# Modulation dot products placed behind residuals and scaled halves, handed out differently, and a softplus on 128 by 192

## The chip, the core and the metric

The kernel runs on one core of one Trainium2 chip. The metric is the device time in microseconds (us) of one execution. A core has TensorE (matrix products, written PE in the profile; PEld is its weight load), VectorE (DVE), ScalarE (ACT), GpSimd (POOL) and SyncE (SP, which here only issues DMAs). Each engine works through its own queue in order.

## The reference, cut to what matters

Two layers work on 384 tokens of width 1024 (128 context tokens, 256 latent ones), all in float32. In outline, for each layer:

```python
shift1, scale1, gate1, shift2, scale2, gate2 = split(silu(c) @ w_ada + b_ada, 6)   # c_ctx for context tokens
h = rms_norm(x, g1) * (1 + scale1) + shift1
z, xbc, dt_raw, p, u, v, gates = split(h @ w_in)
dt = softplus(dt_raw + dt_bias)                  # 2 directions x 32 heads = 64 rows
merged = sum of sigmoid(gate) * branch over (ssd(xbc, dt, z), pool(p), gmlp(u, v))
x = x + gate1 * (merged @ w_out)
h2 = rms_norm(x, g2) * (1 + scale2) + shift2
f_gate, f_up = split(h2 @ w_ffn_in)
x = x + gate2 * ((silu(f_gate) * f_up) @ w_ffn_out)
```

At the end there is one more RMS norm. The state-space scan (ssd) works in chunks of 128 tokens and also returns its final states.

## The kernel before

**Weights.** Every large product takes its weights in keys: blocks of 128 by 1024 floats, 512 KB, stored in the order of use. A key is loaded into one of RB = 6 buffers `raw` (L99), split by ScalarE into a rounded part `whi` (L116) and by VectorE into the rest `wlo` (L117), and used in three matmuls for each product (high by high, high by low, low by high; L166 to L168 where weights stand still, L461 to L463 where tokens do). `Flow.prepare` splits up to LEAD = 3 keys ahead, and `Flow.load` loads as far ahead as the six buffers let it. All loads go through SyncE's queue.

**Modulation.** silu(c) @ w_ada is 6144 columns for each layer. They are worked out as dot products on VectorE. A step is one key of transposed w_ada and two dot products on it (`ada`, L302, one for c_ctx and one for c; the profile calls the output `ajunk`). Eight steps make one of the six sections of a layer (0 shift1, 1 scale1, 2 gate1, 3 shift2, 4 scale2, 5 gate2). Sections 0 and 1 of layer one are worked out at the start by other code; 80 steps are left, and they wait in the list `adaq`. `take(n)` puts the next n steps into the flow of work, between the units of matmuls. Places where it is called:

- the states stage (`ssd`): 12 steps in layer one, 8 in layer two
- the mixers: 13 in layer one, 8 in layer two
- each pair of gate and up products of the FFN (`fi` keys): one step a pair, ten pairs in each half of the FFN
- the FFN's output (`fo` keys), by `between`: one step after each key but the last. Each half of the FFN has two blocks of output columns (q = 0, 1); the first half has 6 keys a block, the second half 5, of which four go as one unit in the last block of layer one.

So steps 1 to 25 lie in layer one's states and mixers, 26 to 35 in the first half of its FFN products, 36 to 45 in the first half of its FFN output, 46 to 55 and 56 to 60 in the second half; 61 to 68 lie in layer two's states, 69 to 76 in its mixers, 77 to 80 in its FFN.

**Order of the queues.** TensorE's order is the order of the program. The queues of the other engines are laid out by the compiler's planner, which goes through planned time and gives each engine the ready instruction of highest priority, by place in the program. `high_priority(offset=20)` moves an instruction forward by 20 places; `residual`, `scaled` and `norm` have it, `prepare` moves by 1. A dot product whose load is planned to have landed can thus be put in front of work that comes earlier in the program but isn't ready in the plan.

**The ends of a block.** After the last key of an output block, `residual` multiplies each of the three 128-token tiles by its gate row (`res`) and adds it to x (`accx`), two VectorE instructions a tile, which also frees the tile's PSUM buffer (four of tag `mm`). `scaled` takes the sum of squares (ScalarE), then a reciprocal root of about ten small VectorE instructions (`ssy`, `ssh`, `rst`), then multiplies x by it in two halves, tile `k`: the first on VectorE (L155), the second on ScalarE. `norm` transposes `k` on TensorE (L405), modulates it (`hf`) and splits it into `hthl`, which the next products read. The norms of tiles 1 and 2 are written into the middle of the first product of the next stage (the FFN's first block, or the second layer's V block).

**dt.** `dt_unit` projects dt. Its weight columns stand twice, so that PSUM rows 0 to 63 and 64 to 127 hold the same 64 rows. The softplus is worked out on rows 0 to 63 of 384 tokens: bias, Abs and Exp on ScalarE, then on VectorE a maximum, a reciprocal (L745), a polynomial of nine products, and the sum `dtt`. The two scans (L762, L763) follow.

Of the kernel before, what the change touches and what calls it, by code (L numbers as in the profile page):

```python
# [1 line left out]

# [1 line left out]

# [7 lines left out]
BF16 = mybir.dt.bfloat16  # L12
I32 = mybir.dt.int32
ACTF = mybir.ActivationFunctionType
ALU = mybir.AluOpType
# [4 lines left out]
D = 1024  # L20
NT = 3
TOK = 384
# [9 lines left out]
CP_G1, CP_G2, CP_CW, CP_CB, CP_DS, CP_GS, CP_PS, CP_GU, CP_DTB, CP_AL, CP_BA = 0, 8, 16, 136, 160, 176, 192, 200, 208, 209, 210  # L32
# [29 lines left out]
class Flow:  # L62


    def __init__(self, tc, nc, wdram, pool):
        self.tc, self.nc, self.wdram, self.pool = tc, nc, wdram, pool
        self.units = []
# [56 lines left out]
class Net:  # L124
    def __init__(self, ctx, tc, io):
        self.ctx, self.tc, self.nc, self.io = ctx, tc, tc.nc, io
        self.late = []
        self.tick = 0


    def t(self, pool, tag, shape, bufs, dtype=F32):
# [13 lines left out]
        self.nc.scalar.activation(out=out, in_=in_, func=func, **kw)  # L145

    def tt(self, out, a, b, op):
        self.nc.vector.tensor_tensor(out=out, in0=a, in1=b, op=op)  # L148

    def stt(self, out, a, s, b, op0, op1):  # L150
        self.nc.vector.scalar_tensor_tensor(out=out, in0=a, scalar=s, in1=b, op0=op0, op1=op1)  # L151

    def ts(self, out, a, s1, op0, s2=None, op1=None):
        if op1 is None:
            self.nc.vector.tensor_scalar(out=out, in0=a, scalar1=s1, scalar2=None, op0=op0)  # L155
        else:
            self.nc.vector.tensor_scalar(out=out, in0=a, scalar1=s1, scalar2=s2, op0=op0, op1=op1)

    def split(self, hi, lo, x):
        self.nc.scalar.copy(out=hi, in_=x)  # L160
# [131 lines left out]
    def ada(self, l, sec):  # L292

        hold = {}

        def step(k):
            def fn(raw):
                if k == 0:
                    hold["m"] = self.t(self.base, f"mod{sec}", [128, KT, 2], 2)
                for n in range(2):  # L300
                    junk = self.t(self.base, "ajunk", [128, D], 1, BF16)
                    self.nc.vector.tensor_tensor_reduce(out=junk, in0=raw, in1=self.crow[:, n, :], scale=0.5, scalar=0.0,  # L302
                                                        op0=ALU.mult, op1=ALU.add, accum_out=hold["m"][:, k, n:n + 1])
                if k == KT - 1:
                    self.ada_end(l, sec, hold["m"])
            return fn

        return [((l, sec), [("ada", l, sec, k)], step(k)) for k in range(KT)]
# [73 lines left out]
    def scaled_(self, i, q):  # L382

        r = self.squares(self.x[:, i, q * 512:(q + 1) * 512], D, ("x", i), q, self.parts)
        if q == 0:
            return
        xn = self.xnorm[i] = self.t(self.pool, "k4", [128, D], 4)
        self.ts(xn[:, 0:512], self.x[:, i, 0:512], r, ALU.mult)
        self.act(xn[:, 512:1024], self.x[:, i, 512:1024], ACTF.Copy, scale=r)

    def norm(self, l, which, i):
# [238 lines left out]
    def ssd(self, l):  # L630
        F = self.flow
        F.add([], lambda: self.ssd_open(l))
        self.main([("dt", l)], lambda w: self.dt_unit(l, w))
        fill = [("u", 0, c) for c in range(KT)] + [("g", br, c) for br in range(3) for c in range(KT)][:3 * KT - ORDER.count("g")]
        def filler(n):
            for _ in range(n):
                if fill:
                    kind, br, c = fill.pop(0)
                    if kind == "u":
                        self.main([("in", l, C_U + 128 * c)], lambda w, c=c: self.u_spill(l, c, w))  # L640
                    else:
                        self.main([("in", l, C_G + D * br + 128 * c)], lambda w, br=br, c=c: self.gate_spill(l, br, c, w))
        for g in range(4):
            self.main([("in", l, C_B + 128 * g)], lambda w, g=g: self.conv_unit(l, 16 + g, w))
            self.main([("in", l, C_C + 128 * g)], lambda w, g=g: self.conv_unit(l, 20 + g, w))
            if g == 0:
                self.post(L_TURN, lambda: self.turn(0))
                self.post(L_TURN2, lambda: self.turn(1))
            self.post(L_CB, lambda g=g: self.cb_unit(l, g))
            filler(FILL[g][0])  # L650
            for t in range(4 * g, 4 * g + 4):
                self.main([("in", l, C_X + 128 * t)], lambda w, t=t: self.conv_unit(l, t, w))
                self.post(L_DEC, lambda t=t: self.decay(l, t))
                self.post(L_XN, lambda t=t: self.xnat(l, t))
                self.post(L_ST, lambda t=t: self.states(l, t))
                self.post(L_Y, lambda t=t: self.ypair(l, t))
                self.take((t % 2 == 1) + (l == 0 and t % 4 == 2))
                self.main([("in", l, C_Z + 128 * t)], lambda w, t=t: self.z_unit(l, t, w))
                if t < 15:
                    filler(FILL[g][1 + t % 4])  # L660
            if g == 3:
                break
            self.post(L_G1, lambda g=g: self.gnorm1(l, g))
            self.post(L_G2, lambda g=g: self.gnorm2(l, g))
            for cc in range(4):
                self.post_main(L_SP + cc, [("brs", l, g, cc)], lambda w, g=g, cc=cc: self.sproj(l, g, cc, w))
        while self.late and len(fill) > T_G1 + T_G2 + T_G3:
            filler(1)
        self.flush_all()
        filler(len(fill) - T_G2 - T_G3)  # L670
        F.add([], lambda: self.gnorm1(l, 3))
        filler(len(fill) - T_G3)
        F.add([], lambda: self.gnorm2(l, 3))
        filler(len(fill))
        F.add([], lambda: [self.th_load(l, 0, c) for c in range(3)])
        for cc in range(4):
            self.main([("brs", l, 3, cc)], lambda w, cc=cc: self.sproj(l, 3, cc, w))
# [53 lines left out]
    def dt_unit(self, l, w):  # L731
        nc, pool = self.nc, self.pool
        cp = self.cp[l][0]
        ps = self.ps("mm")
        self.proj(ps, w)
        zz = self.t(pool, "arg", [128, TOK], 2)[0:64]
        self.act(zz, ps[0:64, 0:TOK], ACTF.Identity, bias=cp[0:64, CP_DTB:CP_DTB + 1])
        e = self.t(pool, "W", [128, 2 * TOK], 2)[0:64, 0:TOK]
        self.act(e, zz, ACTF.Abs)
        self.act(e, e, ACTF.Exp, scale=-1.0)  # L740
        mx = self.t(pool, "arg", [128, TOK], 2)[0:64]
        self.ts(mx, zz, 0.0, ALU.max)
        s = self.t(pool, "wb", [128, TOK], 2)[0:64]
        self.ts(s, e, 2.0, ALU.add)
        nc.vector.reciprocal(out=s, in_=s)  # L745
        self.tt(s, s, e, ALU.mult)
        s2 = self.t(pool, "W", [128, 2 * TOK], 2)[0:64, 0:TOK]
        self.tt(s2, s, s, ALU.mult)
        p = self.t(pool, "ysq", [128, TOK], 1)[0:64]
        self.ts(p, s2, 1.0 / 15, ALU.mult)  # L750
        for n in (13, 11, 9, 7, 5, 3):
            self.stt(p, p, 1.0 / n, s2, ALU.add, ALU.mult)
        self.stt(p, p, 1.0, s, ALU.add, ALU.mult)
        dtt = self.t(pool, "dtt", [64, TOK], 1)
        self.stt(dtt, p, 2.0, mx, ALU.mult, ALU.add)
        ea = self.t(pool, "ea", [64, 1], 1)
        self.act(ea, cp[0:64, CP_AL:CP_AL + 1], ACTF.Exp)
        la = self.t(pool, "ysq", [128, TOK], 1)[0:64]
# [388 lines left out]
    def residual_(self, ps, i, c0, n, rows, o):  # L1147
        t = self.t(self.pool, "res", [128, 512], 2)[:, 0:n]
        self.tt(t, ps[:, o:o + n], rows[SEG[i]][:, c0:c0 + n], ALU.mult)
        xv = self.x[:, i, c0:c0 + n]  # L1150
        self.tt(xv, xv, t, ALU.add)

    def back(self, l):
        F = self.flow
# [12 lines left out]
        for q in range(2):  # L1167
            mid = {M0: lambda: self.norm(l, 1, 0)} if q else {}
# [18 lines left out]
        for half, kn in enumerate((6, 5)):  # L1187
            for f in range(at, at + 2 * kn - (0 if half else 2)):
                self.main([("fi", l, f)], lambda w, f=f: self.ffn_gate(l, f, w))
                if f == 3:  # L1190
                    F.add([], lambda: self.ffn_turn(l))
                self.main([("fi", l, NF + f)], lambda w, f=f: self.ffn_up(l, f, w))
                self.take()
            at = 12
            if half == 0:
                self.ada_until(l, 5)
                F.add([], lambda: setattr(self, "rows", self.gate_rows(l, 1)))
            for q in range(2):
                if half and q and l + 1 < DEPTH:
                    self.ada_until(l + 1, 1)  # L1200
                spans = (1,) * (kn - KL) + (KL,) if half and q else (1,) * kn
                mid = {MF: lambda: self.norm(l + 1, 0, 0)} if half and q and l + 1 < DEPTH else {}
                r0 = 6 * half
                after, last = fo_end(q, half)
                self.block_b([("fo", l, q, r) for r in range(r0, r0 + kn)], spans, lambda k, r0=r0: self.fa[2 * r0 + k], after, mid, last, self.take)

    def ffn_first(self, l, i, ps):

# [206 lines left out]
```

## Time and profile before

| what | value |
|---|---|
| median of 3 runs | 1841.76 us (1840.21 to 1842.12) |
| the profiled execution | 1838.79 us, span from first to last instruction 1837.0 us |
| TensorE | busy 1809.4 us (98% of the span), mean granted clock 0.995 |
| VectorE | busy 1457.3 us (79%) |
| ScalarE | busy 966.1 us (53%) |
| DMA | 341.15 MB, mean 186 GB/s |
| dot products (L302) | 160 of 1224 ns mean, 195.8 us in all |

A busy time is the union of an engine's instructions. Matmuls are pipelined, and each is shown longer than the distance from one start to the next; so how fast TensorE goes is read from that distance, and a busy share near 100% can still hide slow stretches. "[2.58 <-DVE k L155]" behind a row means that the engine was idle 2.58 us before it, until the VectorE instruction of line 155 that wrote k ended.

### The profile page before, as it was taken

Reading aid. Unit: us, or ns where it says so; the run is one execution under the profiler, and the core shown is the slowest. Engines: PE = TensorE matmul, PEld = TensorE weight load, DVE = VectorE, ACT = ScalarE, POOL = GpSimd, SP = SyncE. Lnnn points to the kernel's source line nnn. Section 1 sums busy time; section 2 is a strip of 40 time slices with the busy share of each in tenths; the row PEclk is TensorE's granted clock in tenths of the full one; section 3 lists DMA queues with packets and bytes.
Section 4 is the critical chain, followed back from the end, with each engine's and each line's share of the span. In section 5 each row is a group of like instructions: output and inputs, shape, how many; then the busy total and the mean of one; then the engine's idle time right before and its main releaser. Section 6 shows DMA issues by size and latency. Waiting matters only on the chain.

```text
span 1837.0 us, 28886 instructions
## 1 busy us (share of the span) xinstructions
PE 1809.4 (98%) x10688; PEld 1709.8 (93%) x10688; DVE 1457.3 (79%) x2886; ACT 966.1 (53%) x1905; POOL 0.2 (0%) x4
## 2 busy tenths in 40 slices
PE   8999999999999999999999999999999999999998
PEld 5999999999999889889879999999999997998997
DVE  6899979997979687877668989799977797643545
ACT  4687858584443443223365977675834434432332
POOL 0000000000000000000000000000000000000000
PEclk9999999999999999999999999999999999999999
DMA  9676554645768455765555656455456684544441
GB/s 353 235 247 215 184 192 150 206 127 154 259 203 258 153 184 172 253 196 190 180 172 193 211 170 202 152 177 185 137 170 202 193 276 128 163 161 126 126 127 46
DMA packets 112293, 341.15 MB, mean 186 GB/s; under 512 B 12948, under 2 KB 38420, under 8 KB 112024
## 3 DMA queue, kind: packets, MB, share of 16 engines
q1 hardware_dynamic: 112152, 339.30, 56.9%
q8 instruction: 84, 1.38, 0.3%
q14 instruction: 57, 0.47, 0.1%
HBM read 314.38 MB, written 24.87 MB: 185 GB/s over the span
## 4 chain that ended last, share of the span: by engine, by line
PE 87%; DVE 5%; DMA 4%; issue 2%; ACT 1%; SPq 0%; DVEq 0%; ACTq 0%
PE ps_mm L166 21%; PE ps_mm L168 21%; PE ps_mm L167 21%; PE ps_mm L462 5%; PE ps_mm L461 5%; PE ps_mm L463 5%; DMA raw<-w 3%; PE ps_y L924 3%; DVE wlo L117 1%; DVE ajunk L302 1%; PE ps_st L889 1%; PE ps_tr L871 1%; PE ps_mm L1125 1%; PE ps_mm L576 0%; PE ps_tr L405 0%
## 5 line engine op out<-in xcount | busy, mean ns | idle before, releaser
L116 ACT CAST whi<-raw 128x1024 fp32r<-128x1024 f32 x394 | 413.1, 1050 | 534.8 <-PE ps_mm L167 217.4
L166 PE MATMUL ps_mm<-hthl,whi 128*128 128x384 f32 x1936 | 656.5, 339 | 0.0
L168 PE MATMUL ps_mm<-hthl,wlo 128*128 128x384 f32 x1936 | 651.4, 336 | 2.6 <-DVE wlo L117 2.6
L117 DVE TENSOR_TENSOR wlo<-raw,whi 128x1024 fp32r<-128x1024 f32 x394 | 481.8, 1223 | 214.0 <-ACT whi L116 207.9
L167 PE MATMUL ps_mm<-hthl,whi 128*128 128x384 f32 x1936 | 649.8, 336 | 0.0
L168 PEld LDWEIGHTS ps_mm<-hthl,wlo 128*128 128x128 f32 x1936 | 363.7, 188 | 2.9 <-DVE wlo L117 2.9
L166 PEld LDWEIGHTS ps_mm<-hthl,whi 128*128 128x128 f32 x1936 | 364.1, 188 | 2.3 <-issue 1.5
L167 PEld LDWEIGHTS ps_mm<-hthl,whi 128*128 128x128 f32 x1936 | 363.9, 188 | 0.3
L302 DVE CUSTOM_DVE_ANT_0 ajunk<-raw,crow 128x1024 bf16<-128x1024 f32 x160 | 195.8, 1224 | 36.5 <-DMA raw<-w 35.1
L461 PE MATMUL ps_mm<-whi,ah 128*128 128x512 f32 (+1 forms) x360 | 140.9, 392 | 4.0 <-DVE res L148 3.0
L463 PE MATMUL ps_mm<-whi,al 128*128 128x512 f32 (+1 forms) x360 | 141.1, 392 | 0.0
L462 PE MATMUL ps_mm<-wlo,ah 128*128 128x512 f32 (+1 forms) x360 | 140.1, 389 | 0.0
L151 DVE SCALAR_TENSOR_TENSOR ca<-cin,cw,ca 128x388 f32<-128x388 f32 x192 | 118.9, 620 | 2.0 <-ACT ca L145 1.0
L166 PE MATMUL ps_mm<-ah,whi 128*128 128x384 f32 x288 | 98.1, 341 | 0.0
L167 PE MATMUL ps_mm<-al,whi 128*128 128x384 f32 x288 | 96.8, 336 | 0.3 <-DVE al L148 0.3
L168 PE MATMUL ps_mm<-ah,wlo 128*128 128x384 f32 x288 | 96.6, 335 | 0.0
L166 PE MATMUL ps_mm<-yh,whi 128*128 128x384 f32 x256 | 86.9, 339 | 0.0
L160 ACT CAST ah<-t 128x384 fp32r<-128x384 f32 x72 | 36.8, 511 | 93.9 <-DVE t L151 61.8
L167 PE MATMUL ps_mm<-yl,whi 128*128 128x384 f32 x256 | 86.2, 337 | 0.0
L168 PE MATMUL ps_mm<-yh,wlo 128*128 128x384 f32 x256 | 86.1, 337 | 0.0
L461 PEld LDWEIGHTS ps_mm<-whi,ah 128*128 128x128 f32 x360 | 68.1, 189 | 18.6 <-DVE res L148 3.5
L462 PEld LDWEIGHTS ps_mm<-wlo,ah 128*128 128x128 f32 x360 | 68.0, 189 | 14.6
(257 smaller groups left out, 2456.9 us busy)
## 6 DMA issues: line engine op xcount, KB each, us to landing
raw<-w SPq DMA_DIRECT2D x478, 512.0 KB, 4.2
fb<-fsd SPq DMA_DIRECT2D x32, 768.0 KB, 4.7
thd<-spill SPq DMA_DIRECT2D x48, 192.0 KB
spill<-thd SPq DMA_DIRECT2D x48, 192.0 KB, 4.0
araw<-wa SPq DMA_DIRECT2D x12, 512.0 KB, 7.0
s<-s SPq DMA_DIRECT2D x32, 128.0 KB, 2.0
so<-so SPq DMA_DIRECT2D x32, 128.0 KB, 3.8
k<-gd SPq DMA_DIRECT2D x8, 512.0 KB, 5.2
```

Of the source, the lines that this page charges most:

```text
L116: self.nc.scalar.copy(out=hi, in_=raw)
L117: self.nc.vector.tensor_tensor(out=lo, in0=raw, in1=hi.bitcast(F32), op=ALU.subtract)
L151: self.nc.vector.scalar_tensor_tensor(out=out, in0=a, scalar=s, in1=b, op0=op0, op1=op1)
L160: self.nc.scalar.copy(out=hi, in_=x)
L166: mm(out, lhsT=whi, rhs=xhi, start=first, stop=False)
L167: mm(out, lhsT=whi, rhs=xlo, start=False, stop=False)
L168: mm(out, lhsT=wlo, rhs=xhi, start=False, stop=last)
L302: self.nc.vector.tensor_tensor_reduce(out=junk, in0=raw, in1=self.crow[:, n, :], scale=0.5, scalar=0.0, op0=ALU.mult, op1=ALU.add, accum_o ...
L461: mm(out, lhsT=xh[:, ts], rhs=hi[:, ws], start=(kk == 0), stop=False)
L462: mm(out, lhsT=xh[:, ts], rhs=lo[:, ws], start=False, stop=False)
L463: mm(out, lhsT=xl[:, ts], rhs=hi[:, ws], start=False, stop=(kk == kn - 1))
L924: mm(o, lhsT=lt, rhs=rt, start=(n == 0), stop=(n == steps - 1))
```

## The change

Three things are changed.

1. `residual` and `scaled` note their last VectorE instruction in `self.last`. The two dot products of a step are put into a block `issue_after(self.last.ins)`: the planner must place them behind that instruction in VectorE's queue. It is an order and no wait, since both are on one engine. Steps that come before the first residual (those of layer one's states and mixers) are free as before.
2. In the FFN's output, `between` takes a step at its first call and at each third one after it, no longer at each call. In layer two's states `take` has one more step at every fourth t, as in layer one. The 80 steps are now spread so: 1 to 35 as before; 36 to 39 in layer one's first FFN output (two for each block, where there were five); 40 to 49 with the second half's products; 50 to 52 in its output; 53 to 64 in layer two's states; 65 to 72 in its mixers; 73 to 80 in its FFN's first half.
3. The softplus lies on 128 partitions by 192 tokens: rows 0 to 63 hold the first 192 tokens, rows 64 to 127 the others. The bias is added in two ScalarE instructions, and two ScalarE copies bring the result `dth` back to 64 rows by 384 (`dtt`).

```diff
+        self.last = None
...
-                for n in range(2):
-                    junk = self.t(self.base, "ajunk", [128, D], 1, BF16)
-                    self.nc.vector.tensor_tensor_reduce(out=junk, in0=raw, in1=self.crow[:, n, :], scale=0.5, scalar=0.0,
-                                                        op0=ALU.mult, op1=ALU.add, accum_out=hold["m"][:, k, n:n + 1])
+
+                with self.tc.issue_after(self.last.ins) if self.last is not None else nullcontext():
+                    for n in range(2):
+                        junk = self.t(self.base, "ajunk", [128, D], 1, BF16)
+                        self.nc.vector.tensor_tensor_reduce(out=junk, in0=raw, in1=self.crow[:, n, :], scale=0.5, scalar=0.0,
+                                                            op0=ALU.mult, op1=ALU.add, accum_out=hold["m"][:, k, n:n + 1])
...
-        self.ts(xn[:, 0:512], self.x[:, i, 0:512], r, ALU.mult)
+        self.last = self.ts(xn[:, 0:512], self.x[:, i, 0:512], r, ALU.mult)
...
-                self.take((t % 2 == 1) + (l == 0 and t % 4 == 2))
+                self.take((t % 2 == 1) + (t % 4 == 2))
...
-        zz = self.t(pool, "arg", [128, TOK], 2)[0:64]
-        self.act(zz, ps[0:64, 0:TOK], ACTF.Identity, bias=cp[0:64, CP_DTB:CP_DTB + 1])
-        e = self.t(pool, "W", [128, 2 * TOK], 2)[0:64, 0:TOK]
+
+        HT = TOK // 2
+        zz = self.t(pool, "arg", [128, TOK], 2)[:, 0:HT]
+        for n in range(2):
+            r = slice(64 * n, 64 * n + 64)
+            self.act(zz[r], ps[r, n * HT:(n + 1) * HT], ACTF.Identity, bias=cp[r, CP_DTB:CP_DTB + 1])
+        e = self.t(pool, "W", [128, 2 * TOK], 2)[:, 0:HT]
...
+        dth = self.t(pool, "wb", [128, TOK], 2)[:, 0:HT]
+        self.stt(dth, p, 2.0, mx, ALU.mult, ALU.add)
         dtt = self.t(pool, "dtt", [64, TOK], 1)
-        self.stt(dtt, p, 2.0, mx, ALU.mult, ALU.add)
+        for n in range(2):
+            nc.scalar.copy(out=dtt[:, n * HT:(n + 1) * HT], in_=dth[64 * n:64 * n + 64])
...
-        self.tt(xv, xv, t, ALU.add)
+        self.last = self.tt(xv, xv, t, ALU.add)
...
+                due = [0]
+
+                def between():
+                    due[0] += 1
+                    self.take(due[0] % 3 == 1)
...
-                self.block_b([("fo", l, q, r) for r in range(r0, r0 + kn)], spans, lambda k, r0=r0: self.fa[2 * r0 + k], after, mid, last, self.take)
+                self.block_b([("fo", l, q, r) for r in range(r0, r0 + kn)], spans, lambda k, r0=r0: self.fa[2 * r0 + k], after, mid, last, between)
```

The tiles `mx`, `s`, `s2` and `p` of the softplus change from rows 0 to 63 of 384 to all rows of 192 in the same way; their instructions stay.

## Rows read from the trace of the kernel before

**Rows 1.** Timeline of TensorE where it stands still: start, duration, idle before.
```profile
655.48 1.83 PE L405 MATMUL ps_tr<-ident,k 128*128 128x128 f32 x8 [2.58 <-DVE k L155]
...
754.24 0.50 PE L461 MATMUL ps_mm<-whi,ah 128*128 128x512 f32 x1 [0.95 <-DVE t L151]
...
780.91 0.50 PE L461 MATMUL ps_mm<-whi,ah 128*128 128x512 f32 x1 [3.04 <-DVE res L148]
...
991.39 0.44 PE L168 MATMUL ps_mm<-hthl,wlo 128*128 128x384 f32 x1 [2.62 <-DVE wlo L117]
...
1561.59 1.09 PE L405 MATMUL ps_tr<-ident,k 128*128 128x128 f32 x8 [2.93 <-DVE k L155]
```

**Rows 2.** TensorE behind two gaps and without one: stretch, length, busy (count), granted clock.
```profile
655.48:659.17 3.69, 3.69 (x13) 0.54 0.57 188
780.91:785.31 4.40, 4.40 (x12) 0.62 0.58 223
941.40:943.36 1.96, 1.96 (x14) 1.00 0.59 233
```

**Rows 3.** Dot products (ajunk) inside three root chains: stretch, its length, VectorE's busy time (count).
```profile
648.52:654.92 6.40, 3.60 (x3) 1.00 0.58 187
1554.29:1561.05 6.76, 3.58 (x3) 1.00 0.62 198
937.20:940.13 2.93, 0.00 (x0) 1.00 1.09 380
```

**Rows 4.** Dot products counted from 80 us on; columns as in rows 3.
```profile
80.00:640.00 560.00, 61.12 (x50) 1.00 0.61 196
80.00:776.00 696.00, 107.69 (x88) 1.00 0.61 197
```

**Rows 5.** Timeline of VectorE at layer two's first norm, tile 2.
```profile
943.23 0.41 DVE L157 TENSOR_SCALAR hf<-ps_tr,mod,mod 128x128 f32<-128x128 f32 x1 [2.61 <-ACT hf L145]
```

**Rows 6.** Timeline of VectorE between the two blocks of layer one's first FFN output.
```profile
776.61 1.23 DVE L302 CUSTOM_DVE_ANT_0 ajunk<-raw,crow 128x1024 bf16<-128x1024 f32 x1 [0.32 <-DMA raw<-w]
...
780.17 1.28 DVE L148 TENSOR_TENSOR res<-ps_mm,k 128x512 f32<-128x512 f32 x2
```

**Rows 7.** Timeline of TensorE in layer two's FFN output, 21 matmuls apart.
```profile
1681.66 0.39 PE L461 MATMUL ps_mm<-whi,ah 128*128 128x512 f32 x1
...
1686.47 0.39 PE L461 MATMUL ps_mm<-whi,ah 128*128 128x512 f32 x1
```

**Rows 8.** Stretches: FFN output of layer one, of layer two; busy PE, PEld, DVE, ACT, POOL (count).
```profile
735.00:780.00 45.00, 41.92 (x204) 36.54 (x202) 39.08 (x59) 13.10 (x16) 0.00 (x0) 1.00 0.76 256
1650.00:1690.00 40.00, 40.00 (x184) 33.74 (x183) 16.90 (x19) 11.32 (x12) 0.00 (x0) 1.00 0.42 131
```

**Rows 9.** Timeline of VectorE during dt_unit of layer two.
```profile
975.90 1.23 DVE L302 CUSTOM_DVE_ANT_0 ajunk<-raw,crow 128x1024 bf16<-128x1024 f32 x1 [1.53 <-DMA raw<-w]
...
978.46 2.54 DVE L745 RECIPROCAL wb<-wb 64x384 f32<-64x384 f32 x1
...
984.18 0.54 DVE L151 SCALAR_TENSOR_TENSOR ysq<-ysq,W 64x384 f32<-64x384 f32 x1
...
986.32 0.41 DVE L151 SCALAR_TENSOR_TENSOR bt<-th,ca 128x256 f32<-128x256 f32 x1
...
990.13 1.21 DVE L117 TENSOR_TENSOR wlo<-raw,whi 128x1024 fp32r<-128x1024 f32 x1
```

**Rows 10.** Timeline of ScalarE during dt_unit of layer two.
```profile
972.61 0.57 ACT L145 ACTIVATE arg<-ps_mm,cp 64x384 f32<-64x384 f32 x1
...
976.77 0.26 ACT L791 COPY cin<-ps_mm 128x128 f32<-128x128 f32 x1
976.92 0.38 ACT L792 COPY cin<-ps_mm 128x256 f32<-128x256 f32 x1
```

**Rows 11.** Stretches: the states of layer one, of layer two; columns as in rows 8.
```profile
80.00:490.00 410.00, 409.15 (x2700) 400.28 (x2699) 380.15 (x815) 279.89 (x635) 0.00 (x0) 1.00 0.60 192
990.00:1400.00 410.00, 408.61 (x2697) 400.21 (x2698) 365.25 (x784) 280.33 (x634) 0.00 (x0) 1.00 0.57 184
```

More of the change, by code (lines that the diff above doesn't have):

```diff
@@ L1 @@
-from contextlib import ExitStack
+from contextlib import ExitStack, nullcontext
 import numpy as np
@@ L147, in tt @@
     def tt(self, out, a, b, op):
-        self.nc.vector.tensor_tensor(out=out, in0=a, in1=b, op=op)
+        return self.nc.vector.tensor_tensor(out=out, in0=a, in1=b, op=op)
     def stt(self, out, a, s, b, op0, op1):
@@ L154, in ts @@
         if op1 is None:
-            self.nc.vector.tensor_scalar(out=out, in0=a, scalar1=s1, scalar2=None, op0=op0)
+            return self.nc.vector.tensor_scalar(out=out, in0=a, scalar1=s1, scalar2=None, op0=op0)
         else:
-            self.nc.vector.tensor_scalar(out=out, in0=a, scalar1=s1, scalar2=s2, op0=op0, op1=op1)
+            return self.nc.vector.tensor_scalar(out=out, in0=a, scalar1=s1, scalar2=s2, op0=op0, op1=op1)
     def split(self, hi, lo, x):
@@ L735, in dt_unit @@
         self.proj(ps, w)
-        zz = self.t(pool, "arg", [128, TOK], 2)[0:64]
-        self.act(zz, ps[0:64, 0:TOK], ACTF.Identity, bias=cp[0:64, CP_DTB:CP_DTB + 1])
-        e = self.t(pool, "W", [128, 2 * TOK], 2)[0:64, 0:TOK]
+        HT = TOK // 2
[4 more added lines that the diff above has]
+        e = self.t(pool, "W", [128, 2 * TOK], 2)[:, 0:HT]
         self.act(e, zz, ACTF.Abs)
         self.act(e, e, ACTF.Exp, scale=-1.0)
-        mx = self.t(pool, "arg", [128, TOK], 2)[0:64]
+        mx = self.t(pool, "arg", [128, TOK], 2)[:, 0:HT]
         self.ts(mx, zz, 0.0, ALU.max)
-        s = self.t(pool, "wb", [128, TOK], 2)[0:64]
+        s = self.t(pool, "wb", [128, TOK], 2)[:, 0:HT]
         self.ts(s, e, 2.0, ALU.add)
@@ L746, in dt_unit @@
         self.tt(s, s, e, ALU.mult)
-        s2 = self.t(pool, "W", [128, 2 * TOK], 2)[0:64, 0:TOK]
+        s2 = self.t(pool, "W", [128, 2 * TOK], 2)[:, 0:HT]
         self.tt(s2, s, s, ALU.mult)
-        p = self.t(pool, "ysq", [128, TOK], 1)[0:64]
+        p = self.t(pool, "ysq", [128, TOK], 1)[:, 0:HT]
         self.ts(p, s2, 1.0 / 15, ALU.mult)
```

## The prediction

> **What bounds the kernel now.** I read the page first: TensorE is busy 98% of the span, so the question is where it isn't, and where it runs slowly although busy. The timeline of TensorE answers the first. After the start-up, five places of about a microsecond or more are left [rows 1], and the reader is to see who ends each: the scaled half `k` of tile 2 at the FFN norm of layer one (2.58) and of layer two (2.93), a VectorE product `t` at the start of layer one's FFN output (0.95), a residual between that output's two blocks (3.04), and a `wlo` during layer two's dt unit (2.62). That is 12.1 us, and VectorE ends all five.
>
> The windows of TensorE answer the second. Behind the gap at 655.48, eight transposes and five matmuls take 3.69 at a granted clock of 0.54; the same pieces, where no gap precedes, take 1.96 from 941.40 on at clock 1.00 (the count there has one more, a matmul that was still running) [rows 2]. A matmul of 512 columns follows the last after (1686.47 - 1681.66) / 21 = 0.229 [rows 7], so the slow clock costs 3.69 - 1.96 = 1.73 in the one place, and from 780.91 on 4.40 - 12 x 0.229 = 1.65, at clock 0.62. At full speed both stretches are at the higher of the two levels, 2.4 GHz; the mean below 0.7 says most of them was at 1.2. With 3.4 of slow clock, 15.5 us in all are open to this change.
>
> **Why VectorE is late there.** At the norms, from the start of the root chain to `k` it takes 6.40 and 6.76, with three dot products inside each; where layer two's first norm does the same with none, 2.93 [rows 3], and TensorE has no idle in front of its transposes at 941.40 [rows 2]. Fifty dots, 25 steps, stand before 640 [rows 4], so those in layer one's chain are of steps 26 and 27; in layer two the program puts 76 steps ahead, and they are of 77 and 78. The program has those after the first FFN pairs, and the planner moved them up past the chain. At 780.17 the residuals of the first block start, right behind dots that still waited for their load (0.32 <- DMA at 776.61, [rows 6]); 88 dots stand before 776 [rows 4], so these are step 45, the last of the second block, and the four before it are of that block too. In layer two, whose FFN output has no dots, TensorE is busy 40.00 of 40.00; in layer one 41.92 of 45.00, with VectorE at 39.08 [rows 8].
>
> **Part 1, the order.** Both norm places: steps 26, 27, 77 and 78 come after the last `scaled` in the program, so they now stand behind `k`. Without dots `k` would start 2.93 after its chain [rows 3], that is 6.40 - 2.93 = 3.5 and 6.76 - 2.93 = 3.8 earlier. Both gaps are shorter, so the wait on `k` goes and the clock with it: 2.58 + 1.73 and 2.93. What is late next is `hf` and `hthl` of the same tile: the dots are now ready right behind `k`. VectorE is idle there for 2.61 until 943.23 [rows 5], and two dots of 1.23 [rows 6] fill it just about; a third, or one between `hf` and `hthl`, delays the norm, and TensorE's products of tile 2 with it. I take somewhat over half a dot, 0.7, as left at each place; bounds are 0 and two dots, 2.46. Gain: 3.6 (1.9 to 4.3) and 2.2 (0.5 to 2.9).
>
> The residual at 780.17: the dots of the second block now stand behind it, and `res` can start as soon as its product ends. Gain 3.04 + 1.65 = 4.7; I see no bound below 4, since the number of dots falls as well.
>
> What the order holds up: the dots themselves, and through their `raw` buffer the load six keys later, and through SyncE's queue what is behind that. Six keys of 18 matmuls at 0.229 are 24.7 us of TensorE's work; a step held from one block's middle to the residual waits less. Nothing reads a section early: the last step of layer two's scale1 (48) lies in the ninth of ten pairs of the second half, with nine keys of FFN output, 37 us, between it and the norm that uses it. Cost 0.
>
> **Part 2, where the steps go.** In layer one's FFN output VectorE loses six dot pairs from the first half (ten steps become four) and two from the second. The 0.95 at 754.24 ends with a late `t`; of the dots that fill VectorE from 735 to 780 (39.08 busy [rows 8]) most are of this output's ten steps, and six of the ten go, though a step may still land on the place: 0.8 (0 to 1.0). In layer two's states there are four more steps, 4 x 2 x 1.23 = 9.8 us of VectorE. VectorE was busy there 365.25 of 410, and 380.15 of 410 in layer one with its twelve steps, where TensorE was busy 409.15 [rows 11]. So 375 should hide the same way; I put down a loss of 0.5 (0 to 2.6, one gap like that at 991.39), since section gate1 now ends there, with its transposes on TensorE. The four steps more in layer two's FFN lie where layer one has its ten: 0.
>
> **Part 3, the softplus.** On VectorE a product of 64 by 384 takes 0.54 and one of 128 by 256 takes 0.41 [rows 9], 0.13 for 128 columns, so 128 by 192 takes 0.34: 0.20 saved each, nine in front of the late `wlo` at 990.13: 1.8. The reciprocal took 2.54 for 384 a row; about 0.15 of an instruction is fixed (0.54 - 3 x 0.13), so half the rest, 1.2, goes. The trace has no reciprocal of another size, so its bounds are 0 and 1.27. Together 3.0 (1.8 to 3.3, with 0.2 for the scalar operations) against a gap of 2.62: I take 2.3 (0.5 to 2.6, the lower end if the planner fills the place with another dot like that of 975.90). In layer one nothing waits long at this place: 0.
>
> On ScalarE copies of 128 and 256 columns take 0.26 and 0.38, so 192 take 0.32 [rows 10]. Two bias instructions for one is 0.64 against 0.57; Abs and Exp save some 0.2 each; the two copies add 0.64 and a hand-over in front of the scans. The scans feed SyncE's spill of `fs` and the transposes of `turn`, six units later in the program. ScalarE is busy 280 of 410 [rows 11]. Cost 0; 0.6 if a split of weights had to wait behind the copies.
>
> The Trainium skill, ScalarE: Activation LUTs, section What ACT_TABLE_LOAD costs, speaks against splitting: an ACTIVATE with a bias per partition is said to cost about 280 ns plus 0.833 ns an element, one with immediates 186 ns plus the same, so cutting an instruction in two pays the fixed part twice. The trace agrees for the whole one (0.57 [rows 10], against 0.60). By that page the halves would be an estimated 0.88 and the copies 0.69, half a microsecond more on ScalarE than by the rows; hidden or not, the sum would move by no more than 0.3.
>
> **Sum.** 3.6 + 2.2 + 4.7 + 0.8 - 0.5 + 2.3 = 13.1. The profiled execution took 1838.79, which gives 1825.7; the median shown is 3.0 above it (1841.76), so the median after is 1841.76 - 13.1 = 1828.7. Lower ends of the gains with the upper end of the loss: 1.9 + 0.5 + 4.0 + 0 - 2.6 + 0.5 - 0.6 = 3.7, upper ends 4.3 + 2.9 + 4.7 + 1.0 + 2.6 = 15.5: 1838 to 1826, and beyond 1826 only if small waits elsewhere go too.
>
> **Rivals.**
> - *The stall moves down the norm.* The four dots wait right behind `k` and the planner, which takes whatever is ready, puts two too many in front of `hf` and `hthl`; the softplus finds another `wlo` behind it. For it: before, the planner filled every break of the chain that way. Against: 2.61 of the way is idle. Gains 1.9 + 0.5 + 4.7 + 0.8 - 0.5 + 0.5 = 7.9: 1834. Chance 0.2.
> - *It doesn't do what it says.* The noted instruction is the last in the program, not the late one; if dots in front of `k` belong to steps before it, the order changes nothing there, and the fewer steps alone act: 4.7 + 0.8 + 0.5 = 6.0: 1836. Against: the step numbers above. Chance 0.05.
> - *No change: the ring runs dry.* Held dots hold their buffers, loads behind them start late, and TensorE gets as many new gaps as it lost; three like that at 780.91 with its clock are 14 us: 1842. For it: SyncE's queue is in order. Against: six keys of slack. Chance 0.08.
> - *Slower: VectorE becomes the bound in layer two's states.* Each of the twelve steps there could do what the one at 975.90 does, wait for its load and push a `wlo` late, 2.62 a time. Eleven new ones are 29 us: 1857. It decides from the seventh on (7 x 2.62 = 18.3 against 13.1 and the 0.2%). Against: layer one does it with twelve. Chance 0.07.
>
> **Numbers.** The forecast has 0.6, 1828.7 with its own range 1824 to 1832. A measurement tells about 0.2% from no change, 3.7 us here. Faster by more: 0.6 + 0.2 + 0.05 = 0.85; within: 0.08; slower: 0.07. The range that leaves out no more than 2 in 10 reaches from 1823 to 1836.
>
> **What would show it.** Right: no idle in front of L405 at the FFN norms, and no ajunk in the root chains; no slow clock at 785; TensorE busy 45 of 45 there; dt's `wlo` in time. Wrong: idle in front of L461 a few microseconds behind the transposes, ended by `hthl`; SyncE waiting for ajunk with TensorE idle on `whi`; gaps ended by `wlo` in layer two's states.

## The result and the profile after

| | median | runs | profiled execution | its span |
|---|---|---|---|---|
| before | 1841.94 us | 4, 1840.21 to 1843.17 | 1838.79 | 1837.0 |
| after | 1822.20 us | 4, 1821.59 to 1823.41 | 1821.59 | 1819.8 |

The ratio is 0.9894, with a 95% interval of 0.9877 to 0.9911: faster, by 19.7 us where 13.1 were forecast. The time lies 0.8 below the low end of the range given, so the range missed it.

The waits of TensorE in the kernel after, in total, times, longest:

```profile
PE ps_mm L260 <- DMA posr<-posr: 2.9, 1, 2.9
PE ps_tr L545 <- ACT arow L523: 1.7, 2, 1.2
PE ps_tr L335 <- ACT ysq L961: 0.7, 1, 0.7
PE ps_tr L520 <- DVE st L149: 0.5, 1, 0.5
PE ps_mm L168 <- DVE al L149: 0.3, 2, 0.2
```

The first, second and fourth lie in the start-up; the other two are short and stand in the kernel before as well. None of the five places of [rows 1] is among them. The chain of work that ended last is 97% TensorE's, against 87% before. The transposes of the two FFN norms, L408 now, start without an idle, and a stretch behind them and one behind the change of blocks run at the full granted clock:

```profile
651.75 1.03 PE L408 MATMUL ps_tr<-ident,k 128*128 128x128 f32 x8
...
1544.29 1.03 PE L408 MATMUL ps_tr<-ident,k 128*128 128x128 f32 x8
```

```profile
651.50:653.80 2.30, 2.30 (x16) 1.00 0.00 2
769.00:773.40 4.40, 4.40 (x21) 1.00 0.39 119
```

The columns of this second fence are stretch, length, TensorE's busy time and count, granted clock. In these 4.40 us 19 matmuls start (the count of 21 has two that were still running), where 12 did in [rows 2]. The FFN output and the states, as in [rows 8, 11], TensorE's busy time first, then PEld, VectorE, ScalarE:

```profile
725.60:770.60 45.00, 45.00 (x226) 40.44 (x226) 26.50 (x36) 14.87 (x19) 0.00 (x0) 1.00 0.57 186
...
976.00:1386.00 410.00, 410.00 (x2708) 401.45 (x2707) 372.96 (x802) 281.73 (x638) 0.00 (x0) 1.00 0.58 188
```

VectorE lost 12.6 us of work in the first of these stretches; in layer two's states it has 7.7 more than before, and TensorE is busy throughout. VectorE's timeline at layer one's FFN norm, from the start of the root chain on:

```profile
647.54 0.15 DVE L156 TENSOR_SCALAR ssy<-ssm 128x1 int32<-128x1 int32 x1
...
650.95 0.48 DVE L156 TENSOR_SCALAR k<-accx,ssy 128x512 f32<-128x512 f32 x1
651.34 1.22 DVE L305 CUSTOM_DVE_ANT_0 ajunk<-raw,crow 128x1024 bf16<-128x1024 f32 x1
...
652.60 1.23 DVE L305 CUSTOM_DVE_ANT_0 ajunk<-raw,crow 128x1024 bf16<-128x1024 f32 x1
653.75 0.08 DVE L305 DVE_READ_ACCUMULATOR2_ANT mod<- 128x1 f32 x1
653.75 0.41 DVE L158 TENSOR_SCALAR hf<-ps_tr,mod,mod 128x128 f32<-128x128 f32 x1
654.08 1.22 DVE L305 CUSTOM_DVE_ANT_0 ajunk<-raw,crow 128x1024 bf16<-128x1024 f32 x1
655.22 0.08 DVE L305 DVE_READ_ACCUMULATOR2_ANT mod<- 128x1 f32 x1
655.22 0.69 DVE L149 TENSOR_TENSOR hthl<-hf,hthl 128x512 fp32r<-128x512 f32 x1
655.82 0.41 DVE L158 TENSOR_SCALAR hf<-ps_tr,mod,mod 128x128 f32<-128x128 f32 x1
```

The chain takes 650.95 - 647.54 = 3.41 and has no dot in it (6.40 and three dots in [rows 3]). Two dots follow `k`, and a third stands between `hf` and `hthl`. The two cost TensorE nothing. The third puts the end of `hthl` at 655.22 + 0.69 = 655.91, and the matmul that waits for it starts at 655.96:

```profile
655.66 0.40 PE L465 MATMUL ps_mm<-wlo,hthl 128*128 128x512 f32 x1
655.96 0.50 PE L466 MATMUL ps_mm<-whi,hthl 128*128 128x512 f32 x1
656.30 0.40 PE L464 MATMUL ps_mm<-whi,hthl 128*128 128x512 f32 x1
```

From start to start this is 0.30 and 0.34 where the others take 0.23: 0.18 is lost. The list of waits above has no row for it, since the record of a matmul, 0.39 long, covers the pause. Layer two's FFN norm has the same (1548.19, 1548.51, 1548.85).

In layer two's dt unit, the softplus on VectorE (L752 is the reciprocal) and on ScalarE:

```profile
964.28 1.23 DVE L305 CUSTOM_DVE_ANT_0 ajunk<-raw,crow 128x1024 bf16<-128x1024 f32 x1 [1.12 <-DMA raw<-w]
...
965.43 1.35 DVE L752 RECIPROCAL wb<-wb 128x192 f32<-128x192 f32 x1
966.69 1.16 DVE L117 TENSOR_TENSOR wlo<-raw,whi 128x1024 fp32r<-128x1024 f32 x1
...
970.07 0.35 DVE L152 SCALAR_TENSOR_TENSOR ysq<-ysq,W 128x192 f32<-128x192 f32 x1
```

```profile
961.14 0.84 ACT L146 ACTIVATE arg<-ps_mm,cp 64x192 f32<-64x192 f32 x2
...
976.14 0.72 ACT L765 COPY dtt<-wb 64x192 f32<-64x192 f32 x2 [2.04 <-DVE wb L152]
```

The reciprocal and the products cost what the sum said (1.34 and 0.34). The planner also lays this stretch out anew: one dot of the step, not two, stands in the chain, and a `wlo` right behind the reciprocal. On ScalarE the two bias instructions take 0.84 and the two copies 0.72 together, more than the 0.64 and 0.64 of the sum. The Trainium skill, ScalarE: Activation LUTs, section What ACT_TABLE_LOAD costs, gave an estimated 0.88 and 0.69; the same section lets neighbours overlap by about 93 ns, with which the estimates would be 0.79 and 0.60. This trace is nearer the first. ScalarE had idle for it (2.04 in front of the copies), and nothing on TensorE waits.

### The profile page after: what moved, and what is told of

Same layout as the page of the kernel before. It is cut to its first block, busy times and chain, and to the rows that moved or that the text cites. A ratio compares the mean times of both kernels' runs of the same rounds, so it can differ in the third digit from the quotient of the medians.

```text
span 1819.8 us, 28901 instructions
## 1 busy us (share of the span) xinstructions
PE 1805.4 (99%) x10688; PEld 1707.3 (94%) x10688; DVE 1447.6 (80%) x2886; ACT 968.9 (53%) x1911; POOL 0.2 (0%) x4
## 4 chain that ended last, share of the span: by engine, by line
PE 97%; DVE 1%; ACT 1%; issue 0%; DMA 0%; SPq 0%; DVEq 0%; ACTq 0%
PE ps_mm L167 23%; PE ps_mm L169 23%; PE ps_mm L168 23%; PE ps_mm L465 6%; PE ps_mm L466 6%; PE ps_mm L464 6%; PE ps_y L934 3%; PE ps_st L899 1%; PE ps_tr L881 1%; PE ps_mm L1135 1%; PE ps_mm L579 0%; PE ps_mm L581 0%; PE ps_mm L580 0%; PE ps_st L901 0%; PE ps_st L900 0%
## 5 line engine op out<-in xcount | busy, mean ns | idle before, releaser
L466 PEld LDWEIGHTS ps_mm<-whi,al 128*128 128x128 f32 x360 | 67.6, 188 | 14.8
```

The costliest lines, as they stand in the source:

```text
L466: mm(out, lhsT=xl[:, ts], rhs=hi[:, ws], start=False, stop=(kk == kn - 1))
```

## Experiments

### The three parts alone

Each part was put on the kernel before by itself. The order:

```diff
+                with self.tc.issue_after(self.last.ins) if self.last is not None else nullcontext():
...
+        self.last = self.ts(xn[:, 0:512], self.x[:, i, 0:512], r, ALU.mult)
...
+        self.last = self.tt(xv, xv, t, ALU.add)
```

> Part 1 alone: residual and scaled note their last instruction and the dot products stand behind it; the steps are handed out as before and the softplus is the old one. Theory A (each part takes away its own waits, and nothing is given back): the two FFN norms give 4.4 and 3.1, the wait between the blocks of layer one's first FFN output gives 4.8; the 0.9 at the start of that output and the 2.9 in layer two's dt stay. Gain 12.3 us, ratio 0.993. Theory B (the ring runs dry): with five steps of the second block held, not two, the loads behind them come late, and the FFN output gives back what it gained: gain 7.5 us or less, ratio 0.996, with TensorE idle on whi or wlo between 780 and 805.

Measured: 1826.21 us median (1825.44 to 1827.01, 5 runs), against 1839.88 for the kernel before on the same chip (23 runs, 1836.67 to 1844.79, shared by the first four experiments). Ratio 0.9924 (0.9910 to 0.9939). Theory A holds, and a little more: the 0.95 at the start of the output went too. All of TensorE's waits that are left with over 1 us in total:

```profile
PE ps_mm L260 <- DMA posr<-posr: 2.9, 1, 2.9
PE ps_mm L169 <- DVE wlo L117: 2.2, 1, 2.2
PE ps_tr L519 <- DVE st L152: 1.2, 1, 1.2
PE ps_tr L544 <- ACT arow L522: 1.1, 2, 0.6
```

The one of 2.2 is dt's in layer two, the others lie in the start-up. The five steps of the second block, ten dots, now all run behind the residuals; TensorE in the output before and after that point:

```profile
772.00:791.00 19.00, 19.00 (x84) 1.00 0.71 217
725.00:770.00 45.00, 45.00 (x227) 1.00 0.66 216
```

It is busy at the full clock, so the loads behind the held dots come in time: the ring does not run dry, even with five steps held.

The steps handed out differently:

```diff
-                self.take((t % 2 == 1) + (l == 0 and t % 4 == 2))
+                self.take((t % 2 == 1) + (t % 4 == 2))
...
+                def between():
+                    due[0] += 1
+                    self.take(due[0] % 3 == 1)
```

> Part 2 alone: fewer steps in the FFN's output, four more in layer two's states; no order, old softplus. Theory A: the FFN output loses its two waits, 4.8 and 0.9, the norms and dt keep theirs, the states of layer two cost nothing: gain 5.7 us, ratio 0.997. Theory B (only the order keeps the residual free): the two steps of the second block are still moved up in front of the residual, wait for their loads there, and the gap of about 3 us with its slow clock stays: gain 1 us, ratio 0.9995.

Measured: 1832.68 us median (1829.17 to 1839.56, 12 runs), ratio 0.9965 (0.9952 to 0.9977). Theory A, 7.2 us for an expected 5.7. Fewer dots remove the two waits of the FFN output by themselves; the norms and dt keep theirs (the profiled execution, 1837.47, is the second slowest of the twelve):

```profile
PE ps_tr L405 <- DVE k L155: 6.2, 2, 3.6
PE ps_mm L168 <- DVE wlo L117: 3.0, 1, 3.0
```

The softplus:

```diff
-        zz = self.t(pool, "arg", [128, TOK], 2)[0:64]
-        self.act(zz, ps[0:64, 0:TOK], ACTF.Identity, bias=cp[0:64, CP_DTB:CP_DTB + 1])
+        zz = self.t(pool, "arg", [128, TOK], 2)[:, 0:HT]
+        for n in range(2):
+            r = slice(64 * n, 64 * n + 64)
+            self.act(zz[r], ps[r, n * HT:(n + 1) * HT], ACTF.Identity, bias=cp[r, CP_DTB:CP_DTB + 1])
```

> Part 3 alone: the softplus on 128 by 192. Theory A: layer two's dt loses its wait of 2.9 us and layer one's 0.5: gain 3.4 us, ratio 0.998. Theory B (it was the free dot product of layer two, not the softplus): the wait at the weights' rest stays in part, gain 1 us or less.

Measured: 1836.78 us median (1835.07 to 1841.49, 12 runs), ratio 0.9985 (0.9975 to 0.9995): 3.1 us, Theory A. The wait on `wlo` is gone from layer two's dt, and with it a short one in layer one's, where transposes waited for `ct` (from the first of them to the next product it is 88.42 to 89.50 before, 87.86 to 88.45 in the full change: 0.49 less); at layer two's first states a new one of 0.2 stands, ended by ScalarE's copy `dtc`.

The three gains, 13.7 + 7.2 + 3.1 = 24.0, are more than the whole: the FFN output's waits, 1.2 and 4.9 by the starts of matmuls (table below), are counted in the first two. Counted once they leave 17.9. The 19.7 of the result is more than that because its four executions of before lie high in a wide spread: their median of 1841.94 is 2 us above the 1839.88 of the 23 here and the 1839.98 of 13 more on another chip.

### The order and the softplus without the new handing out

The kernel of the first experiment with the softplus of the third.

> Parts 1 and 3 without part 2: the order and the narrow softplus, the steps handed out as before (ten in each first FFN output, eight in layer two's states). Theory A: the order alone had no idle left in the FFN output, so part 2 is worth nothing: 1822 us, the time of the full change, within 0.1%. Theory B: part 2 gives what the sum put down for it, 0.8 at the start of the output less 0.5 in the states, or more in executions that the profile did not catch: 1823 to 1825 us.

Measured: 1822.46 us median (1821.87 to 1823.07, 4 runs) against 1839.98 for the kernel before on the same chip (13 runs, 1836.94 to 1843.73, shared with the three experiments that follow), ratio 0.9907 (0.9892 to 0.9922): 17.5 us, and the time of the full change. Theory A: behind the order, part 2 has nothing left to remove, and it costs nothing.

### The residual noted, the scaled half not

Against the kernel of the first experiment:

```diff
         xn = self.xnorm[i] = self.t(self.pool, "k4", [128, D], 4)
-        self.last = self.ts(xn[:, 0:512], self.x[:, i, 0:512], r, ALU.mult)
+        self.ts(xn[:, 0:512], self.x[:, i, 0:512], r, ALU.mult)
```

> Part 1 with only the residual noted, not the scaled half; nothing else. Theory A (it is the note at the scaled half that frees the norms, the one at the residual that frees the output's second block): dots stand again in the root chains, both FFN norms keep their waits of about 2.7 us, and the wait between the blocks goes: gain 5 to 6 us, ratio 0.997. Theory B (the residual's note is enough, since it holds the dots back long enough): gain 12 us or more, ratio 0.993.

Measured: 1834.71 us median (1832.67 to 1837.17, 10 runs) against 1839.98, ratio 0.9971 (0.9961 to 0.9981): 5.3 us, Theory A. The dots come back, three into the root chain of each FFN norm, and both norms wait again, while the wait on `res` is gone:

```profile
PE ps_tr L407 <- DVE k L156: 5.4, 2, 2.9
...
PE ps_mm L169 <- DVE wlo L117: 2.5, 1, 2.5
```

So the two notes do two things: the scaled half's frees the norms, the residual's the output.

### Twice the dots at the norms

In the full change, each dot of the gate2 sections is worked out twice, the second time into the same place:

```diff
-                    for n in range(2):
+                    for n in (0, 1) * (2 if sec == 5 else 1):
```

> The full change, with each dot product of the gate2 sections (steps 25 to 32 and 73 to 80) worked out twice, so that eight dots instead of four are ready behind the scaled half at each FFN norm. Theory A (the norm took four dots for nothing because VectorE's idle behind the scaled half, 2.61 us, holds two of them, and the next is hidden while ScalarE works; more dots find the same breaks, one a break): no idle of TensorE at the norms, time within 0.1% of the full change. Theory B (the charge of the prediction was right in kind, and four was just the number that fits): a further dot falls in front of the norm's second half or of its rest, and TensorE waits 0.5 to 2.5 us at each norm: 1 to 5 us slower than the full change.

Measured: 1822.94 us median (1822.72 to 1823.29, 4 runs), ratio 0.9909 (0.9892 to 0.9926). Theory A: within 0.1% of the full change. Behind `k` the planner used the same breaks for as many dots as in the full change, four (VectorE's dots in the 12 us of layer one's norm, busy and count):

```profile
652.00:664.00 12.00, 4.87 (x4) 1.00 0.33 94
```

The other four of the eight come later. 32 dots more, 39 us of VectorE's work, cost the kernel nothing that can be measured.

### Dots held behind the old softplus

The kernel of the first experiment, with one more note:

```diff
-        self.stt(dtt, p, 2.0, mx, ALU.mult, ALU.add)
+        self.last = self.stt(dtt, p, 2.0, mx, ALU.mult, ALU.add)
```

> Part 1, and the dot products also held behind the old softplus (its last product is noted too); the softplus stays on 64 by 384, the steps as before. Against the run with the order alone this tells whether the wait in layer two's dt came from the free dot products or from the softplus. Theory A (the dots: two of them and the wait for their load, 4 us, stand in the chain): the wait of 2.4 us with its slow clock goes, 1822 to 1823 us. Theory B (the softplus itself is too long): the wait stays or only shrinks to a microsecond, 1824 to 1826 us.

Measured: 1822.49 us median (1822.24 to 1823.30, 4 runs), ratio 0.9908 (0.9893 to 0.9922). Theory A: the wait on `wlo` goes with the softplus still on 64 by 384. The `wlo` now stands right behind the reciprocal:

```profile
964.06 2.54 DVE L747 RECIPROCAL wb<-wb 64x384 f32<-64x384 f32 x1
966.53 1.15 DVE L117 TENSOR_TENSOR wlo<-raw,whi 128x1024 fp32r<-128x1024 f32 x1
```

With the order alone it came behind the whole chain of products:

```profile
967.02 2.54 DVE L747 RECIPROCAL wb<-wb 64x384 f32<-64x384 f32 x1
...
978.67 1.22 DVE L117 TENSOR_TENSOR wlo<-raw,whi 128x1024 fp32r<-128x1024 f32 x1
```

So the old softplus is not too long by itself. That its shortening alone is enough is not shown: in the third experiment, as in the full change, the planner also took one of the two dots out of the chain and put a `wlo` right behind the reciprocal (975.54 and 976.80 there). In both ways the `wlo` is early; which of length, dots and order would do by itself was not separated.

### The kernel before once more

> The kernel before once more, for its profile. The median fell by 2.5 us more than the two profiled executions differ. Theory A: the waits of before cost a different amount in each execution, since TensorE's granted clock falls behind some of them in one execution and not in another; then this profile has the same five idle places of the same length, but slow clock behind other ones of them, and a span that differs by 1 to 3 us from 1837.0. Theory B: the difference is spread over the execution, or lies at its start: then the clock behind the five places is as it was.

Measured: one run of 1841.6 us, span 1839.7, where the first profile had 1838.79 and 1837.0. Theory A in its main point: the five places are the same, and what they cost is not. TensorE's waits:

```profile
PE ps_tr L405 <- DVE k L155: 5.1, 2, 2.6
PE ps_mm L461 <- DVE res L148: 4.8, 1, 4.8
...
PE ps_mm L168 <- DVE wlo L117: 2.5, 1, 2.5
```

Behind dt's gap in layer two, TensorE in this execution, by stretch, length, busy time and count, granted clock:

```profile
991.44:995.94 4.50, 4.50 (x17) 0.62 0.63 182
```

and in the first profile of the same kernel:

```profile
991.39:995.94 4.55, 4.55 (x28) 1.00 0.60 180
```

An idle of 2.50 was followed by slow clock, one of 2.62 was not. That the waits kept their length was wrong for two places: `res` took 4.8, not 3.0, and `t` 0.3, not 1.0.

## Why the prediction was right in direction and too small

**What was right.** The five places, who ended each, and that the change removes all five. The order frees the norms (twice the scaled half's note) and the second block of the FFN output; dt's wait goes; the dots of layer two's states stay hidden; the sizes on VectorE (1.35 for 1.34, 0.35 for 0.34); no ring that runs dry. None of the rivals came in its size; of the first, the stall that moves down the norm, there is 0.18 at each.

**The step that failed** is the sizes in the sum, and the time that the sum was taken from: together 6.5 us between 1828.7 and 1822.2. The two profiled executions run the same 10688 matmuls, in the same order but for two. How much earlier one and the same matmul starts therefore tells what each place gave; each row has a matmul behind the place:

| behind | starts before | starts after | earlier by | the place gave | forecast |
|---|---|---|---|---|---|
| the start-up | 70.07 | 69.50 | 0.57 | 0.6 | 0 |
| layer one's dt | 89.94 | 88.88 | 1.06 | 0.5 | 0 |
| layer one's FFN norm | 662.20 | 657.00 | 5.20 | 4.1 | 3.6 |
| the start of its FFN output | 754.58 | 748.15 | 6.43 | 1.2 | 0.8 |
| the change of blocks there | 785.57 | 774.24 | 11.33 | 4.9 | 4.7 |
| layer two's dt and states | 1200.02 | 1185.82 | 14.20 | 2.9 | 2.3 - 0.5 |
| layer two's FFN norm | 1700.20 | 1683.04 | 17.16 | 3.0 | 2.2 |

That is 17.2 in all for a forecast of 13.1: 4.1 of the 6.5. The other 2.4 is the time it was taken from.

- *Charges for what comes next: 2.4 taken off, 0.5 found.* 15.5 us were found open, 13.1 forecast. The difference is 0.7 at each norm, 0.5 in the states, 0.3 and 0.15 at dt and the output. The charge at the norms was the largest: "I take somewhat over half a dot, 0.7, as left at each place". The profile after shows two dots in the 2.61 of idle that [rows 5] had, and one more between `hf` and `hthl`, as the prediction says; but that one is hidden while ScalarE works on its part of `hthl` (654.46 to 655.11; VectorE's starts at 655.22), up to the 0.18. The run with twice the dots showed that the planner puts in no more. In the states 0.1 is left (14.34 earlier at dt's end, 991.67 against 977.33; 14.20 from 1200.02 on).
- *Left out of the sum: 2.2.* Idle is measured to the modelled end of a matmul, 0.39 long where the next follows after 0.23, so each of the five gaps was some 0.16 longer, 0.8 in all. The first matmul behind a gap is followed late as well (754.24 to 754.58 is 0.34, not 0.23): some 0.1 at each of the three gaps where no slow clock was summed, 0.3. Layer one's dt had the short wait on `ct`, 0.5, that went with the narrow softplus; it was put at 0. The start-up gave 0.6, and that is chance: the tenth large matmul starts at 21.03 before, 20.45 after, and at 20.42 in the second profile of before. Against this, the slow clock of [rows 2] was taken 0.1 too dear, since the stretch of 1.96 ends before the next matmul starts at 943.44; 2.04 is right, and 3.69 - 2.04 = 1.65.
- *The time it was taken from: 2.4.* The prediction took its gain off a median of three executions, 3.0 above the profiled one. After, the profiled execution lies 0.6 below the median. The three lay high in a wide spread: over 23 and 13 further executions the median of before is 1839.88 and 1839.98, 1.1 above the profile. From there the same sum gives 1826.8, and the gain on one chip, with the order and the narrow softplus, is 17.5 and not 19.7.

The second profile of before shows what the spread comes from in large part. Behind a gap of these two executions slow clock costs 1.4 to 1.7 us, where it comes (by the starts of the same matmuls at full clock); the first profile had it behind two gaps, the second behind four (granted clock 0.58, 0.66, 0.62 and 0.82 over the 3.5 to 4.5 us behind them), and the wait on `res` was 1.8 longer there. Of the 36 executions the twelve with a mean granted clock of 0.997 or more have a median of 1838.3, the nine with 0.994 or less one of 1843.2. The number of gaps alone does not set the spread: the run with the steps alone has three of them left and spreads over 10.4 us in 12 executions, the kernel before over 8.1 in 23. The four kernels that have none of the five left spread over 0.6 to 1.8, in 4 executions each.

One slip changes nothing: the prediction's half microsecond more on ScalarE is 0.3 (0.88 + 0.69 against 0.64 + 0.64).

**Where the parts stand.** Part 2 was put down as +0.8 - 0.5. By itself it gives 7.2; behind part 1 nothing. The 4.7 of the residual was credited to the order, and either part gives it. Of the softplus the gain was 2.9 with the states, and the two free dots, not its length alone, made the wait: holding them back does the same.

**What stays open.** Why the wait on `t` at the start of the FFN output is 1.0, 0.3 or nothing in kernels that have the same dots there was not settled; which gap is followed by slow clock was only observed; and at dt, what moved the `wlo` forward was not taken apart.

## What to carry to other kernels

A planner that fills an engine's breaks with ready work of low priority can put it in front of a short chain that the bound engine waits for. Naming the last instruction of such a chain and queueing the filler behind it cost nothing here and kept the filler's use of the breaks; moving the filler elsewhere gave the same only at the chain that it was moved away from. When a gap of the bound engine is removed, count with it the slow clock of the average execution, for which one profile or three executions aren't enough. Read what a gap costs from start to start, and charge for the next wait only what a row shows to be without a break.

## What the runs showed of the hardware

The same gap of TensorE, of about 2.5 us in the same place of the same kernel, left the granted clock at 1.00 in one execution and at 0.62 over the next 4.5 us in another. The kernel with five such gaps spreads over 8.1 us in 23 executions; with only this one of them left, the order alone spreads over 1.6 in five.

Two ACTIVATEs on 64 by 192 with a bias took 0.84 together where one on 64 by 384 took 0.57; a reciprocal took 2.54 on 64 by 384 and 1.35 on 128 by 192.
